# Attention scores as plain float32 products on the two row halves of the array

## The chip, the cores and the metric

The kernel runs on 1 core of one Trainium2 chip. The metric is the device time of one execution in microseconds (us). Most executions of a kernel agree within 0.3%. An engine here means one of TensorE (PE, matrix products; PEld is its weight load), VectorE (DVE), ScalarE (ACT), GpSimd (POOL); SP issues the large DMA transfers.

## The reference, cut to what matters

One layer of a hybrid backbone over 512 latent tokens of width 1024, with 256 context tokens. After an adaLN-modulated RMSNorm, one input projection feeds three groups of heads side by side: neighbourhood attention (8 heads of 64 dims), a Hyena mixer and a Conformer convolution module. Their outputs are concatenated, projected and added to the stream. Then follows a mixture of 16 experts in which every expert picks its 64 tokens.

```python
h  = modulate(rmsnorm(x, norm1_g), sh1, sc1)
q, k, v, hy_in, cf_in = split(h @ w_in)
kc, vc = split(modulate(rmsnorm(ctx, norm1_g), csh1, csc1) @ w_in[:, D_NA:3 * D_NA])
# per head, one softmax of a latent query over its grid window and all 256 context keys
s_nb = where(mask, einsum('bqhd,bkhd->bhqk', q, k) * 64 ** -0.5 + bias, -1e30)
s_cx = einsum('bqhd,bkhd->bhqk', q, kc) * 64 ** -0.5
p    = softmax(concat([s_nb, s_cx]))
attn = p[..., :nk] @ v + p[..., nk:] @ vc
x = x + g1 * (concat([attn, hyena(hy_in), conformer(cf_in)]) @ w_out)
h2 = modulate(rmsnorm(x, norm2_g), sh2, sc2)
x = x + g2 * expert_choice_ffn(h2, router_w, w1, w3, w2)     # w1, w3: 1024 x 2048, w2: 2048 x 1024, 16 experts
return rmsnorm(x, final_norm_g)
```

## The kernel before

The program runs once through these stages: adaLN vectors and norms; the projections for Hyena, the Conformer module, queries, values and keys, with the Hyena filter and the depthwise convolution beside them; attention, with the output projection of the other two groups as filler; the rest of the output projection, the second norm and the routing; 16 experts, whose weights (384 loads of 1 MB) come through a pool of 22 buffers of 1 MB (`U`); the final norm.

**Products in three parts.** Weights and activations are float32. For the projections each operand is split into a high part rounded to `float32r` and a low part, the rest; `mm3` (L547 to L550) then issues hi·hi, lo·hi and hi·lo, each one pass. `split` (L510) makes the parts of a weight block: ACT rounds (`wh`, L515), POOL or, for listed pieces, DVE subtracts (`wl`, L516). The experts' products (L1306, L1307, L1346) and the scatter product `pZ` (L1204) are plain float32: the compiler makes two matmul records of each.

**Queries and keys.** `evac_q` takes the projected queries out of the accumulation bank: per block m of two heads, ACT rounds each half of the rows (one head of 64 dims), scaled by -1/8, and DVE writes the rest to the *other* half of the rows (L727, L728). So the 128 rows of one head's stationary operand are its high and its low part. `dup_k` does the like for keys: ACT writes the high part to both halves of the rows (L733, L734), DVE the low part (L735). Keys take four buffers `KK` and one `kcl`, queries two `Q`.

**Scores.** `scores(hp, b, s)` makes the scores of one head (pair hp, half s) for 128 queries (block b): a matmul of 128 rows (high and low query against the doubled high key) and one of 64 rows (high query against low key), once for the 256 window keys and once for the 256 context keys: four matmuls (L946 to L949). Then DVE adds the bias and finds the minimum (L954), ACT takes exp with the sum (L957), DVE divides (L958, L959). `ptrans` transposes the 128x512 block in four matmuls into `pT` (L965) and copies it out as `PT`, in turn on ACT and DVE; `av` multiplies with the values into `pO` (L976) and splits the result into `mixh` (ACT, L980) and `mixl` (DVE, L981).

**What sets the order.** Around the attention the PE, ACT and DVE orders come from the scheduler of the tile framework, which places the program's instructions by its own estimate of when each can run and by the pools: four accumulation banks `psA` (projections `pP`, scores `pS`, output projection `pX`), two `psT`, two `psY`. The generator `attention` walks over 32 heads, two heads ahead of the transposes, and lets `out_part` fill in; from there on a string of words (L1140 in the kernel before) says when each step of the output projection, the routing and the rest of the attention is issued. SP's loads stand in one queue, in program order; a load that waits for its buffer holds up all loads behind it. `w_out` comes in four blocks: `load_wo(0, 1)` is called among the key products, `load_wo(n, 0)` multiplies the block by the gate on DVE (L880, four instructions of 128x512 each), and its attention half is used last. In the same stretch DVE runs the depthwise convolution as 60 multiply-adds (`glu`, L590); the copies of the context values (`vc`, L105) and the low parts of the key weights stand in the same DVE queue.

Of the kernel before, what the change touches and what calls it, by code (L numbers as in the profile page):

```python
# [9 lines left out]
FT = mybir.dt.float32  # L10
# [35 lines left out]
TYPE = [0, 1, 1, 2]  # L46
# [4 lines left out]
def hybrid_kernel(ctx: ExitStack, tc: tile.TileContext, a, out: bass.AP):  # L51
# [24 lines left out]
    def free(k=1, keep=0):  # L76
        used[0] -= k
        pump(keep)

    def free_only(k=1):  # L80
        used[0] -= k

    def psA(name="psA"):
        return psum.tile([128, 512], FT, name=name, tag="A", bufs=4)
# [7 lines left out]
    def W(name="w", dt=FT):  # L92
        if name in ("g", "aff2", "lists", "od", "sn", "u", "xo", "sig", "sq", "dg", "arg", ):
            return early.tile([128, 512], dt, name=name, tag="w", bufs=2)
        return work.tile([128, 512], dt, name=name, tag="w")
# [40 lines left out]
    def small_t(name, n, dt=FT, bufs=4):  # L136
        return work.tile([128, n], dt, name=name, tag=name, bufs=bufs)
# [28 lines left out]
    def take(key):  # L166
        while key not in ready:
            assert loads and used[0] < NU, key
            go = loads.popleft()
            if go is not None:  # L170
                go()
        return ready.pop(key)
# [337 lines left out]
    def split(raw, keep, dve=()):  # L510
        hi = U("wh", FR)
        lo = U("wl", FR)
        for i in range(4):
            s = slice(i * 512, (i + 1) * 512)
            nc.scalar.activation(hi[:, s], raw[:, s], AF.Copy)  # L515
            (nc.vector if i in dve else nc.gpsimd).tensor_sub(lo[:, s], raw[:, s], hi[:, s].bitcast(FT))  # L516
        free(1, keep)
        return hi, lo
# [200 lines left out]
    HALF = [slice(0, 64), slice(64, 128)]  # L719

    def evac_q(m, ps):
        if m % 2 == 0:
            Q.append(U("Q", FR))
        for s in range(2):
            r, o = HALF[s], HALF[1 - s]
            c = slice((2 * (m % 2) + s) * 512, (2 * (m % 2) + s + 1) * 512)
            nc.scalar.activation(Q[-1][r, c], ps[r], AF.Copy, scale=-0.125)  # L727
            nc.vector.scalar_tensor_tensor(Q[-1][o, c], ps[r], -0.125, Q[-1][r, c].bitcast(FT), op0=OP.mult, op1=OP.subtract)  # L728

    def dup_k(hi, lo, ps):  # L730
        for s in range(2):
            r, o = HALF[s], HALF[1 - s]
            nc.scalar.activation(hi[s][r], ps[r], AF.Copy)  # L733
            nc.scalar.activation(hi[s][o], ps[r], AF.Copy)  # L734
            nc.vector.tensor_sub(lo[r], ps[r], hi[s][r].bitcast(FT))  # L735

    def evac_k(m, ps):
        t = KK[m]
        dup_k([t[:, 0:512], t[:, 512:1024]], t[:, 1024:1536], ps)

    def evac_v(b, ps):
        if b == 0:
# [106 lines left out]
    def fetch_bias(hp):  # L849
        for s in range(2):  # L850
            rb[hp, s] = g = W("g")[:, 0:8 * RPBW]
            src = bass.AP(tensor=rp.tensor, offset=rp.offset + (2 * hp + s) * 15 * RPBW,
                          ap=[[1, 16], [RPBW, 8], [1, 7 * RPBW + 48]])
            nc.gpsimd.dma_start(g[:, 0:7 * RPBW + 48], src)
# [10 lines left out]

    parts = []
    for u in range(2):
        parts.append([t.rearrange("p (k n) -> p k n", n=512) for t in split(take(("win", "k", u)), 5, DVE_LO.get(("k", u), ()))])
    fetch_bias(0)
    build_tm(0)  # L870
    fetch_bias(1)
# [16 lines left out]
    for u in range(2):  # L888
        hi, lo = parts[u]
        if u:  # L890
            KK.extend([U("KK", FR) for _ in range(4)])
            kcl = U("kcl", FR)[:, 0:1024].rearrange("p (m n) -> p m n", n=256)
        for ctx_ in (True, False):
            for m in range(4):
                s = slice(m * 128, (m + 1) * 128)
                for k in range(4):
                    kg = 4 * u + k
                    mm3((psc if ctx_ else pss)[m], (hi[:, k, s], lo[:, k, s]),
                        (ch(kg), cl(kg)) if ctx_ else (hh(kg), hl(kg)), kg == 0, kg == 7)
                if u and ctx_:  # L900
                    dup_k([KK[m][:, 1536:1792], KK[m][:, 1792:2048]], kcl[:, m], psc[m])
                elif u:
                    evac_k(m, pss[m])
            if u and ctx_:
                free_only(2)
                load_wo(0, 1, 2)
        if u == 0:
            free_only(2)
# [27 lines left out]
    idxf = p1[0:16, 0:128].rearrange("e (i n) -> e i n", i=2)  # L936
    rsT = small.tile([128, 4], FT, name="rsT")

    def scores(hp, b, s):
        r = HALF[s]  # L940
        qt, kk = Q[hp // 2], KK[hp]
        q0 = (2 * (hp % 2) + s) * 512 + 128 * b
        q = qt[:, q0:q0 + 128]
        k0 = 8 * KB[b]
        ps = psA("pS")
        mm(ps[:, 0:256], q, kk[:, s * 512 + k0:s * 512 + k0 + 256], start=True, stop=False)  # L946
        mm(ps[:, 0:256], q[r], kk[r, 1024 + k0:1024 + k0 + 256], start=False, stop=True)
        mm(ps[:, 256:512], q, kk[:, 1536 + 256 * s:1792 + 256 * s], start=True, stop=False)
        mm(ps[:, 256:512], q[r], kcl[r, hp], start=False, stop=True)  # L949
        p = W("P")  # L950
        i = 2 * TYPE[b] + s
        m2 = small_t("m2", 4, bufs=6)

        nc.vector.tensor_tensor_reduce(out=p.rearrange("p (a n) -> p a n", a=2), in0=ps.rearrange("p (a n) -> p a n", a=2),  # L954
                                       in1=TM[hp][:, i:7:6 - i], scale=1.0, scalar=3e38,
                                       op0=OP.add, op1=OP.min, accum_out=m2[:, 0:1])
        nc.scalar.activation(p, p, AF.Exp, scale=-1.0, bias=m2[:, 0:1], accum_out=m2[:, 1:2])  # L957
        nc.vector.reciprocal(m2[:, 2:3], m2[:, 1:2])  # L958
        nc.vector.tensor_scalar(p, p, m2[:, 2:3], None, op0=OP.mult)  # L959
        return p  # L960

    def ptrans(p):
        t = psT("pT")
        for i in range(4):
            nc.tensor.transpose(t[:, i * 128:(i + 1) * 128], p[:, i * 128:(i + 1) * 128], ident)  # L965
        pt = W("PT")
        copy(pt, t)
        return pt
# [13 lines left out]

    def attention():
        ps = deque()
        pend = deque()
        steps = [(hp, b, s) for hp in range(2) for b in range(4) for s in range(2)]
        steps += [(hp, b, s) for b in range(4) for hp in (2, 3) for s in range(2)]
        parts = [out_part(0), out_part(1)]
        build_tm(1)
        fetch_bias(2)  # L990
        for i in range(len(steps) + 2):
            if i < len(steps):
                ps.append(scores(*steps[i]))
            for _ in range(2):
                if i < 8:
                    next(parts[0])
                elif 9 <= i < 17:
                    next(parts[1])
            if i >= 2:
                hp, b, s = steps[i - 2]  # L1000
                pend.append(ptrans(ps.popleft()))
                if s == 1:
                    av(b, hp, [pend.popleft(), pend.popleft()])
                    if b == 3:
                        free(2 + hp % 2, PK[hp])
                        if hp < 2:
                            build_tm(hp + 2)
                        if hp == 0:
                            fetch_bias(3)
                        if hp == 1:  # L1010
                            load_wo(0, 0, 2)
                            load_wo(1, 0, PK[4])
            if i == 7:
                finish(parts[0])
                free_only(2)
                load_wo(1, 1, PK[5])
            if i == 16:
                finish(parts[1])
                free_only(4)
            yield  # L1020

    def out_proj(n, b):
# [94 lines left out]
    limit[0] = 99  # L1117
    att = attention()
    ada3 = adaln(3)
    for i in range(26):  # L1120
        next(att)
        if i in (21, 21, 22, 25):
            next(ada3)

    def steps(g, at):
# [11 lines left out]
    left = lambda b: one(x_rows, b, 0)  # L1137
    go = lambda *g: [next(i, None) for i in g]
    op = {(n, b): out_proj(n, b) for n in range(2) for b in range(4)}
    for w in "p00 l0 p10 a a r0 a a p11 p01 r0 l1 r1 r0 r1 a p02 p12 q13 r1 r2 q13 r1 r0 a a q03 l2 q03 a f p13 r2 p03 r2 l3 r3 r3 r2 r3 r3".split():  # L1140
        if w == "a":
            go(att)
        elif w == "f":
            finish(att)
            free(3, 0)
        elif w[0] == "p":
            finish(op[int(w[1]), int(w[2])])
        elif w[0] == "q":
            go(op[int(w[1]), int(w[2])])
        elif w[0] == "l":  # L1150
            go(left(int(w[1])))
        elif w[0] == "r":
            go(rt[int(w[1])])
# [315 lines left out]
```

## Time and profile before

| quantity | value |
|---|---|
| median of 3 runs | 1385.86 us (1385.47 to 1389.58) |
| profiled execution | 1391.59 us, span 1389.8 us |
| mean granted TensorE clock in it | 0.958 of full speed |
| PE busy | 1280.8 us (92%) |
| DVE, ACT, POOL busy | 494.5, 229.6, 155.5 us |
| bytes moved by DMA | 458.02 MB |

The profile is of one execution. A busy PE is not PE at its peak: the records of matmuls overlap, so the time of one is read from the start of one record to the start of the next, or from the chain of waits. The granted clock is a share of 2.4 GHz; 0.5 is the lower level, 1.2 GHz. By place in the span: projections to about 268 us, attention from 268 to about 405 us, routing to about 432 us, experts to 1340 us, the final norm after that.

### The profile page before, as it was taken

How to read it: one execution, taken by the hardware profiler on the slowest of the kernel's cores; microseconds unless marked ns; L12 is line 12 of the kernel's file. 1: busy time of each engine (PE TensorE's matmuls, PEld its weight loads, DVE VectorE, ACT ScalarE, POOL GpSimd, SP SyncE). 2: the span in 40 equal slices, each digit the busy share in tenths (PEclk: the TensorE clock that was granted, in tenths of full speed). 3: DMA queues.
4: the chain of work that ended last, by engine and by line, in shares of the span. 5: the costliest groups of instructions: out<-in, count | busy, mean ns of one | idle time of the engine just before them, and what ended most of it. 6: DMA issues, size and time to landing. Idle time of an engine off the chain costs nothing.

```text
span 1389.8 us, 15284 instructions
## 1 busy us (share of the span) xinstructions
PE 1280.8 (92%) x6148; PEld 625.6 (45%) x6148; DVE 494.5 (36%) x991; ACT 229.6 (17%) x477; POOL 155.5 (11%) x166
## 2 busy tenths in 40 slices
PE   6998888999988998998999999899899889989987
PEld 2576566776663335334333433533433353343323
DVE  6777997485464111112112121211212121121214
ACT  3532232743440101000000000100000010000002
POOL 2333443455020000000000000000000000000000
PEclk9999998997999997998999899899999989999999
DMA  9835022432457996999999999999999999999996
GB/s 354 339 145 188 31 65 80 120 120 91 181 214 303 416 414 259 416 421 414 417 417 414 421 413 421 415 417 418 414 421 414 419 416 417 417 415 421 414 419 268
DMA packets 89365, 458.02 MB, mean 330 GB/s; under 512 B 7364, under 2 KB 9228, under 8 KB 54478
## 3 DMA queue, kind: packets, MB, share of 16 engines
q1 hardware_dynamic: 88046, 453.64, 81.1%
q0 software_dynamic: 912, 3.06, 0.9%
q8 instruction: 48, 0.79, 0.2%
q10 hardware_dynamic: 336, 0.35, 0.1%
q14 instruction: 23, 0.19, 0.0%
HBM read 453.87 MB, written 2.36 MB: 328 GB/s over the span
## 4 chain that ended last, share of the span: by engine, by line
PE 70%; DVE 13%; DMA 11%; ACT 3%; issue 2%; POOLq 0%; DVEq 0%; ACTq 0%; SPq 0%
PE pa L1306 26%; PE py L1346 13%; DMA ld<-in_w_dram 10%; PE pT L1194 7%; PE pZ L1204 4%; DVE glu L590 4%; PE pT L1333 2%; PE pO L976 2%; PE pa L1307 1%; PE pP L550 1%; PE pP L549 1%; PE pP L548 1%; PE pM L431 1%; PE pT L965 1%; PE pX L548 1%
## 5 line engine op out<-in xcount | busy, mean ns | idle before, releaser
L1307 PE MATMUL pa<-ld,xh 128*64 128x512 f32 x1024 | 455.5, 595 | 10.2 <-DMA ld<-in_w_dram 10.2
L1306 PE MATMUL pa<-ld,xh 128*64 128x512 f32 x1024 | 455.8, 595 | 0.3 <-DVE xh L1088 0.3
L1306 PEld LDWEIGHTS pa<-ld,xh 128*64 128x64 f32 x1024 | 135.0, 137 | 262.2 <-issue 256.1
L1346 PE MATMUL py<-ld,xh 128*64 128x512 f32 x1024 | 225.0, 597 | 0.0
L1207 DVE TENSOR_TENSOR acc<-acc,pZ 128x512 f32<-128x512 f32 x112 | 72.0, 684 | 307.2 <-PE pZ L1204 307.2
L1307 PEld LDWEIGHTS pa<-ld,xh 128*64 128x64 f32 x1024 | 134.9, 137 | 47.7 <-issue 26.5
L1346 PEld LDWEIGHTS py<-ld,xh 128*64 128x64 f32 x1024 | 72.5, 138 | 141.1 <-issue 137.5
L103 ACT ACTIVATE au<-pa 128x512 f32<-128x512 f32 x32 | 19.1, 597 | 641.6 <-PE pa L1307 641.6
L1194 PE MATMUL pT<-ohg,ld 128*128 128x128 f32 x512 | 95.8, 347 | 31.1 <-DVE xh L1088 15.1
L1373 POOL DMA_INDIRECT out_dram<-yg,where x1 | 1.1, 1115 | 953.0 <-DVE yg L1372 953.0
L1194 PEld LDWEIGHTS pT<-ohg,ld 128*128 128x128 f32 x512 | 82.5, 242 | 48.2 <-DVE xh L1088 21.7
L1350 DVE SCALAR_TENSOR_TENSOR yg<-py,ig,g1bc 128x512 f32<-128x512 f32 x16 | 12.0, 752 | 206.6 <-PE py L1346 206.6
L516 POOL TENSOR_TENSOR wl<-ld,wh 128x512 fp32r<-128x512 f32 x44 | 62.7, 1454 | 95.6 <-ACT wh L515 71.3
L1204 PE MATMUL pZ<-yg,oh 64*128 64x512 f32 x240 | 68.9, 641 | 1.5 <-DVE acc L1207 1.5
L548 PE MATMUL pP<-hh,wh 128*128 128x512 f32 x144 | 60.3, 420 | 7.8 <-DVE vc L105 6.6
L549 PE MATMUL pP<-hl,wh 128*128 128x512 f32 x144 | 58.9, 410 | 1.5 <-DVE hl L507 1.5
L550 PE MATMUL pP<-hh,wl 128*128 128x512 f32 x144 | 57.6, 410 | 2.7 <-DVE wl L516 2.7
L590 DVE SCALAR_TENSOR_TENSOR glu<-glu,p 128x512 f32<-128x512 f32 x60 | 57.9, 965 | 1.1
L1333 PE MATMUL pT<-c,au 128*128 128x128 f32 x256 | 41.8, 292 | 12.3 <-DVE acc L1207 5.4
L1088 DVE TENSOR_SCALAR xh<-pT,A,B 128x128 f32<-128x128 f32 x32 | 13.1, 410 | 106.5 <-PE pT L1194 106.5
L105 DVE COPY au<-pa 128x512 f32<-128x512 f32 x32 | 22.1, 692 | 76.0 <-PE pa L1307 72.9
L1333 PEld LDWEIGHTS pT<-c,au 128*128 128x128 f32 x256 | 28.6, 146 | 29.9 <-DVE xh L1336 13.1
(345 smaller groups left out, 1371.9 us busy)
## 6 DMA issues: line engine op xcount, KB each, us to landing
ld<-in_w_dram SPq DMA_DIRECT2D x384, 1024.0 KB, 19.8
ld<-in_w_mod_dram SPq DMA_DIRECT2D x24, 1024.0 KB, 11.4
ld<-in_w_in_dram SPq DMA_DIRECT2D x11, 1024.0 KB, 6.3
ld<-in_w_out_dram SPq DMA_DIRECT2D x4, 1024.0 KB, 9.0
ld<-in_x_dram SPq DMA_DIRECT2D x2, 1024.0 KB, 12.7
ld<-in_x_dram SPq DMA_DIRECT2D x4, 512.0 KB, 7.0
out_dram<-acc SPq DMA_DIRECT2D x4, 512.0 KB, 9.9
g<-in_rpb_dram POOLq DMA_DIRECT2D x8, 244.5 KB, 3.6
```

The lines of the kernel that those rows point to most:

```text
L516: (nc.vector if i in dve else nc.gpsimd).tensor_sub(lo[:, s], raw[:, s], hi[:, s].bitcast(FT))
L548: mm(ps, l[0], r[0], start=start, stop=False)
L549: mm(ps, l[0], r[1], start=False, stop=False)
L550: return mm(ps, l[1], r[0], start=False, stop=stop)
L590: nc.vector.scalar_tensor_tensor(yc[i], glt[i][:, j:j + 512], cw[:, i, j:j + 1], yc[i], op0=OP.mult, op1=OP.add)
L1194: mm(pk, xblk(b)[:, k * 128:(k + 1) * 128], g[:, b * 128:(b + 1) * 128], start=(b == 0), stop=(b == 3))
L1204: mm(ps[h], oh[pr, 128 * c:128 * c + 128], yg[pr], start=True, stop=True)
L1207: nc.vector.tensor_add(ablk(c)[:, s], (ablk if e else xblk)(c)[:, s], ps[h])
L1306: mm(pa[f][0:64], xT[:, k, cs], w1[:, s], start=(k == 0), stop=(k == 7))
L1307: mm(pa[f][64:128], xT[:, k, cs], w3[:, s], start=(k == 0), stop=(k == 7))
L1333: nc.tensor.transpose(p[:, i * 128:(i + 1) * 128], au[f][:, i * 128:(i + 1) * 128], ident)
L1346: mm(py[64 * h:64 * h + 64], hT[:, f], w2[:, i * 1024 + 512 * h:i * 1024 + 512 * h + 512], start=(f == 0), stop=(f == 15))
```

## The change

Queries are copied out once, as plain float32, by ACT (four instructions of 128x512). Keys are copied once per block of two heads, window keys and context keys, by `copy`, which takes ACT and DVE in turn. The two heads of a pair lie on the two halves of the rows of these tiles. The scores of a pair are two plain float32 matmuls, each with 64 rows and 512 columns (256 window keys and 256 context keys through one strided operand), one on each half of the rows. `attention` walks over 16 pairs instead of 32 heads, one pair ahead of the transposes. Q takes one buffer instead of two, KK two instead of four, `kcl` is gone; the counts of buffers freed and kept follow. Softmax, transposes and the products with the values are as before.

```diff
     def evac_q(m, ps):
-        if m % 2 == 0:
-            Q.append(U("Q", FR))
-        for s in range(2):
-            r, o = HALF[s], HALF[1 - s]
-            c = slice((2 * (m % 2) + s) * 512, (2 * (m % 2) + s + 1) * 512)
-            nc.scalar.activation(Q[-1][r, c], ps[r], AF.Copy, scale=-0.125)
-            nc.vector.scalar_tensor_tensor(Q[-1][o, c], ps[r], -0.125, Q[-1][r, c].bitcast(FT), op0=OP.mult, op1=OP.subtract)
-
-    def dup_k(hi, lo, ps):
-        for s in range(2):
-            r, o = HALF[s], HALF[1 - s]
-            nc.scalar.activation(hi[s][r], ps[r], AF.Copy)
-            nc.scalar.activation(hi[s][o], ps[r], AF.Copy)
-            nc.vector.tensor_sub(lo[r], ps[r], hi[s][r].bitcast(FT))
-
-    def evac_k(m, ps):
-        t = KK[m]
-        dup_k([t[:, 0:512], t[:, 512:1024]], t[:, 1024:1536], ps)
+        if m == 0:
+            Q.append(v512(U("Q")))
+        nc.scalar.activation(Q[0][:, m], ps, AF.Copy, scale=-0.125)
+
+    kat = lambda m: KK[m // 2][:, 768 * (m % 2):768 * (m % 2) + 768]
...
-            KK.extend([U("KK", FR) for _ in range(4)])
-            kcl = U("kcl", FR)[:, 0:1024].rearrange("p (m n) -> p m n", n=256)
+            KK.extend([U("KK") for _ in range(2)])
...
-                    dup_k([KK[m][:, 1536:1792], KK[m][:, 1792:2048]], kcl[:, m], psc[m])
+                    copy(kat(m)[:, 512:768], psc[m])
                 elif u:
-                    evac_k(m, pss[m])
+                    copy(kat(m)[:, 0:512], pss[m])
...
-    def scores(hp, b, s):
-        r = HALF[s]
-        qt, kk = Q[hp // 2], KK[hp]
-        q0 = (2 * (hp % 2) + s) * 512 + 128 * b
-        q = qt[:, q0:q0 + 128]
+    def scores(hp, b):
+
         k0 = 8 * KB[b]
-        ps = psA("pS")
-        mm(ps[:, 0:256], q, kk[:, s * 512 + k0:s * 512 + k0 + 256], start=True, stop=False)
-        mm(ps[:, 0:256], q[r], kk[r, 1024 + k0:1024 + k0 + 256], start=False, stop=True)
-        mm(ps[:, 256:512], q, kk[:, 1536 + 256 * s:1792 + 256 * s], start=True, stop=False)
-        mm(ps[:, 256:512], q[r], kcl[r, hp], start=False, stop=True)
...
+        o = 768 * (hp % 2) + k0
+        kk = KK[hp // 2][:, o:o + 2 * (512 - k0)].rearrange("p (a n) -> p a n", a=2)[:, :, 0:256]
+        pss = [psA("pS") for _ in range(2)]
+        for s in range(2):
+            mm(pss[s].rearrange("p (a n) -> p a n", a=2), Q[0][HALF[s], hp, 128 * b:128 * b + 128], kk[HALF[s]],
+               start=True, stop=True)
...
-        steps = [(hp, b, s) for hp in range(2) for b in range(4) for s in range(2)]
-        steps += [(hp, b, s) for b in range(4) for hp in (2, 3) for s in range(2)]
+        steps = [(hp, b) for hp in range(2) for b in range(4)] + [(hp, b) for b in range(4) for hp in (2, 3)]
...
-        for i in range(len(steps) + 2):
+        for i in range(len(steps) + 1):
...
-                        free(2 + hp % 2, PK[hp])
...
+                    free((1, 2, 1, 3)[hp], PK[hp])
```

The change also moves instructions. On PE, at the start of the attention (`pP` are the last key products, `pX` the output projection that fills in), there stand before the four matmuls of a head:

```order
719 L550 MATMUL pP<-hh,wl 128x512
720 L946 MATMUL pS<-KK,Q 128x256
721 L947 MATMUL pS<-KK,Q 128x256
722 L948 MATMUL pS<-KK,Q 128x256
723 L949 MATMUL pS<-kcl,Q 128x256
724 L548 MATMUL pX<-wh,mixh_1177 128x512
```

and after it a pair of heads in one row of two:

```order
724 L550 MATMUL pP<-hh,wl 128x512
725 L932 MATMUL pS<-KK,Q 128x512 x2
726 L548 MATMUL pX<-wh,mixh_1174 128x512
727 L549 MATMUL pX<-wl,mixh_1174 128x512
728 L550 MATMUL pX<-wh,mixl_1175 128x512
729 L548 MATMUL pX<-wh,mixh_1174 128x512
```

Ten of the 16 pairs stand so, both matmuls in a row; of the other six, the two matmuls stand apart, with other products between them.

On DVE, at the end of the depthwise convolution (`glu`) and before the key products, there stand before:

```order
222 L590 SCALAR_TENSOR_TENSOR glu<-glu,p_70 128x512 x11
223 L105 COPY vc_1476<-pC 128x512
224 L590 SCALAR_TENSOR_TENSOR glu<-glu,p_70 128x512 x2
225 L516 TENSOR_TENSOR wl<-ld,wh 128x512
226 L590 SCALAR_TENSOR_TENSOR glu<-glu,p_70 128x512
227 L516 TENSOR_TENSOR wl<-ld,wh 128x512
```

and after:

```order
211 L590 SCALAR_TENSOR_TENSOR glu<-glu,p_70 128x512 x12
212 L105 COPY vc_1463<-pC 128x512
213 L516 TENSOR_TENSOR wl<-ld,wh 128x512
214 L590 SCALAR_TENSOR_TENSOR glu<-glu,p_70 128x512
215 L459 COPY mT<-pT 128x4x4
216 L516 TENSOR_TENSOR wl<-ld,wh 128x512
```

Of the four multiply-adds that stood behind the copy of `vc`, three now stand ahead of it, and the eight L728 that stood earlier in this queue are gone.

On DVE, around the first softmaxes (L954 before, L940 after, is the bias and the minimum; L880 before, L867 after, multiplies `w_out` by the gate), there stand before, behind the first three L954:

```order
267 L735 TENSOR_TENSOR KK<-pP,KK 64x512
268 L958 RECIPROCAL m_1999<-m_1999 128x1
269 L958 RECIPROCAL m_2016<-m_2016 128x1
270 L959 TENSOR_SCALAR P<-P,m_1999 128x512
271 L959 TENSOR_SCALAR P<-P,m_2016 128x512
272 L880 TENSOR_TENSOR ld<-ld,g1bc 128x512
273 L954 ISA P,m_2044<-pS,tm 128x512
```

and after:

```order
237 L562 TENSOR_TENSOR mixl_1175<-glu,mixh_1174 128x512 x2
238 L105 COPY KK<-pC 128x256
239 L105 COPY KK<-pP 128x512
240 L867 TENSOR_TENSOR ld<-ld,g1bc 128x512 x8
241 L105 COPY KK<-pP 128x512
242 L940 ISA P,m_1932<-pS,tm 128x512
```

The eight gate products now stand in one row ahead of the first softmax, instead of spread over the first heads.

## Rows read from the trace of the kernel before

**Rows 1.** The page: busy time of PE, and the chain that ended last.
```profile
PE 1280.8 (92%) x6148; PEld 625.6 (45%) x6148; DVE 494.5 (36%) x991; ACT 229.6 (17%) x477; POOL 155.5 (11%) x166
PE 70%; DVE 13%; DMA 11%; ACT 3%; issue 2%; POOLq 0%; DVEq 0%; ACTq 0%; SPq 0%
```

**Rows 2.** Stretches: busy us (instructions) per engine; then clock, DMA share, GB/s.
```profile
150.00:230.00 80.00, 64.90 (x315) 47.55 (x313) 78.81 (x119) 24.90 (x48) 36.54 (x30) 0.98 0.25 76
230.00:270.00 40.00, 39.59 (x208) 33.48 (x208) 18.26 (x42) 18.19 (x33) 7.96 (x12) 0.92 0.24 52
...
230.00:240.00 10.00, 9.86 (x39) 8.09 (x40) 5.76 (x10) 0.00 (x0) 0.00 (x0) 0.69 0.00 0
...
270.00:330.00 60.00, 59.36 (x318) 41.45 (x318) 44.64 (x97) 30.66 (x69) 36.84 (x40) 1.00 0.36 118
330.00:346.00 16.00, 16.00 (x68) 9.44 (x70) 8.08 (x19) 3.37 (x9) 10.89 (x9) 0.56 0.36 147
346.00:405.00 59.00, 58.91 (x377) 39.97 (x375) 27.19 (x79) 24.04 (x64) 8.40 (x30) 0.98 0.39 146
430.00:440.00 10.00, 8.93 (x46) 4.95 (x48) 4.29 (x20) 0.46 (x1) 1.05 (x1) 1.00 0.24 94
550.00:1340.00 790.00, 742.18 (x3436) 291.80 (x3432) 144.08 (x264) 47.08 (x104) 0.00 (x0) 0.97 1.02 417
```

**Rows 3.** Waits of PE from 150 to 275 us: total, times, longest.
```profile
PE pP L548 <- DVE vc L105: 6.6, 1, 6.6
```

**Rows 4.** DVE in order of time, 215 to 263 us: start, length, line, idle before.
```profile
217.24 12.24 DVE L590 SCALAR_TENSOR_TENSOR glu<-glu,p 128x512 f32<-128x512 f32 x11
229.40 0.68 DVE L105 COPY vc<-pC 128x512 f32<-128x512 f32 x1
...
233.98 1.28 DVE L516 TENSOR_TENSOR wl<-ld,wh 128x512 fp32r<-128x512 f32 x2
...
260.52 2.12 DVE L562 TENSOR_TENSOR mixl<-glu,mixh 128x512 fp32r<-128x512 f32 x2 [1.91 <-ACT mixh L561]
```

**Rows 5.** Query and key splits: min/median/max ns, first to last start us.
```profile
L728 DVE SCALAR_TENSOR_TENSOR Q<-pP,Q x8: 683/685/694, 168.5 to 190.9; 64x512 fp32r<-64x512 f32 x8
L735 DVE TENSOR_TENSOR KK<-pP,KK x8: 682/688/695, 254.7 to 279.1; 64x512 fp32r<-64x512 f32 x8
```

**Rows 6.** The chain of waits from 330 to 346 us: start, us.
```profile
331.54 0.31 PE pS L947
...
332.32 0.51 PE pS L949
```

**Rows 7.** PE in order of time: two of `pX`, then scatter products of experts.
```profile
308.23 0.39 PE L548 MATMUL pX<-wh,mixh 128*128 128x512 f32 x1
308.46 0.40 PE L549 MATMUL pX<-wl,mixh 128*128 128x512 f32 x1
...
497.43 1.13 PE L1204 MATMUL pZ<-yg,oh 64*128 64x512 f32 x4
498.49 0.64 PE L1306 MATMUL pa<-ld,xh 128*64 128x512 f32 x1
...
1338.44 1.72 PE L1204 MATMUL pZ<-yg,oh 64*128 64x512 f32 x4 [0.77 <-DVE acc L1207]
```

**Rows 8.** The chain of waits from 225 to 310 us: one float32 matmul alone.
```profile
238.56 0.86 PE pL L598 x2
```

**Rows 9.** Softmax and gate products: min/median/max ns, first to last start.
```profile
L954 DVE CUSTOM_DVE_ANT_1 P<-pS,tm x28: 672/680/692, 271.9 to 397.3; 128x512 f32<-128x512 f32 x28
L957 ACT ACTIVATE P<-P,m x32: 708/717/727, 275.8 to 402.6; 128x512 f32<-128x512 f32 x32
L959 DVE TENSOR_SCALAR P<-P,m x32: 477/487/1549, 276.8 to 403.6; 128x512 f32<-128x512 f32 x32
L880 DVE TENSOR_TENSOR ld<-ld,g1bc x8: 665/684/1267, 281.0 to 303.5; 128x512 f32<-128x512 f32 x8
```

**Rows 10.** DMA issues: count, KB each, median us to landing.
```profile
ld<-in_w_out_dram SPq DMA_DIRECT2D x4, 1024.0 KB, 9.0
```

More of the change, by code (lines that the diff above doesn't have):

```diff
@@ L867, in hybrid_kernel @@
     for u in range(2):
-        parts.append([t.rearrange("p (k n) -> p k n", n=512) for t in split(take(("win", "k", u)), 5, DVE_LO.get(("k", u), ()))])
+        parts.append([t.rearrange("p (k n) -> p k n", n=512) for t in split(take(("win", "k", u)), 2, DVE_LO.get(("k", u), ()))])
     fetch_bias(0)
@@ L937, in hybrid_kernel @@
     rsT = small.tile([128, 4], FT, name="rsT")
-    def scores(hp, b, s):
-        r = HALF[s]
-        qt, kk = Q[hp // 2], KK[hp]
-        q0 = (2 * (hp % 2) + s) * 512 + 128 * b
-        q = qt[:, q0:q0 + 128]
-        k0 = 8 * KB[b]
-        ps = psA("pS")
-        mm(ps[:, 0:256], q, kk[:, s * 512 + k0:s * 512 + k0 + 256], start=True, stop=False)
-        mm(ps[:, 0:256], q[r], kk[r, 1024 + k0:1024 + k0 + 256], start=False, stop=True)
-        mm(ps[:, 256:512], q, kk[:, 1536 + 256 * s:1792 + 256 * s], start=True, stop=False)
-        mm(ps[:, 256:512], q[r], kcl[r, hp], start=False, stop=True)
[L950 to L960, printed above, removed]
@@ new lines, in scores @@
+    def scores(hp, b):
+        k0 = 8 * KB[b]
+        o = 768 * (hp % 2) + k0
[4 more added lines that the diff above has]
+               start=True, stop=True)
+        out = []
+        for s, ps in enumerate(pss):
+            p = W("P")
+            i = 2 * TYPE[b] + s
+            m2 = small_t("m2", 4, bufs=6)
+            nc.vector.tensor_tensor_reduce(out=p.rearrange("p (a n) -> p a n", a=2), in0=ps.rearrange("p (a n) -> p a n", a=2),
+                                           in1=TM[hp][:, i:7:6 - i], scale=1.0, scalar=3e38,
+                                           op0=OP.add, op1=OP.min, accum_out=m2[:, 0:1])
+            nc.scalar.activation(p, p, AF.Exp, scale=-1.0, bias=m2[:, 0:1], accum_out=m2[:, 1:2])
+            nc.vector.reciprocal(m2[:, 2:3], m2[:, 1:2])
+            nc.vector.tensor_scalar(p, p, m2[:, 2:3], None, op0=OP.mult)
+            out.append(p)
+        return out
@@ L984, in attention @@
         ps = deque()
-        pend = deque()
-        steps = [(hp, b, s) for hp in range(2) for b in range(4) for s in range(2)]
-        steps += [(hp, b, s) for b in range(4) for hp in (2, 3) for s in range(2)]
+        steps = [(hp, b) for hp in range(2) for b in range(4)] + [(hp, b) for b in range(4) for hp in (2, 3)]
         parts = [out_part(0), out_part(1)]
@@ L990, in attention @@
         fetch_bias(2)
-        for i in range(len(steps) + 2):
+        for i in range(len(steps) + 1):
             if i < len(steps):
                 ps.append(scores(*steps[i]))
-            for _ in range(2):
-                if i < 8:
+            for _ in range(4):
+                if i < 4:
                     next(parts[0])
-                elif 9 <= i < 17:
+                elif 5 <= i < 9:
                     next(parts[1])
[L999 to L1004, printed above, removed]
-                        free(2 + hp % 2, PK[hp])
[L1006 to L1013, printed above, removed]
+            if i == 8:
+                finish(parts[1])
+                free_only(4)
+            if i >= 1:
+                hp, b = steps[i - 1]
+                av(b, hp, [ptrans(p) for p in ps.popleft()])
+                if b == 3:
+                    free((1, 2, 1, 3)[hp], PK[hp])
+                    if hp < 2:
+                        build_tm(hp + 2)
+                    if hp == 0:
+                        fetch_bias(3)
+                    if hp == 1:
+                        load_wo(0, 0, 2)
+                        load_wo(1, 0, PK[4])
+            if i == 3:
                 finish(parts[0])
@@ L1016, in attention @@
                 load_wo(1, 1, PK[5])
-            if i == 16:
-                finish(parts[1])
-                free_only(4)
             yield
@@ L1119, in hybrid_kernel @@
     ada3 = adaln(3)
-    for i in range(26):
+    for i in range(13):
         next(att)
-        if i in (21, 21, 22, 25):
+        if i >= 10:
             next(ada3)
@@ L1139, in hybrid_kernel @@
     op = {(n, b): out_proj(n, b) for n in range(2) for b in range(4)}
-    for w in "p00 l0 p10 a a r0 a a p11 p01 r0 l1 r1 r0 r1 a p02 p12 q13 r1 r2 q13 r1 r0 a a q03 l2 q03 a f p13 r2 p03 r2 l3 r3 r3 r2 r3 r3".split():
+    for w in "p00 l0 p10 a r0 a p11 p01 r0 l1 r1 r0 r1 a p02 p12 q13 r1 r2 q13 r1 r0 q03 l2 q03 a f p13 r2 p03 r2 l3 r3 r3 r2 r3 r3".split():
         if w == "a":
@@ L1144, in hybrid_kernel @@
             finish(att)
-            free(3, 0)
+            free(2, 0)
         elif w[0] == "p":
```

## The prediction

> **What bounds the kernel now.** I read the page first: PE is busy for 92% of the span and holds 70% of the chain that ended last, DVE 13%, DMA 11% [rows 1]. That is an average, so the table of stretches comes next [rows 2]. It shows four regimes. From 150 to 230 us DVE is busy 78.81 of 80 us and PE 64.90: DVE bounds. From 230 to 405 us PE is busy nearly throughout (39.59 of 40, 59.36 of 60, 16.00 of 16, 58.91 of 59), at full clock but for 330 to 346, where 0.56 was granted, about the lower level: PE bounds. At 430 to 440 the DMA share falls to 0.24: the buffers are full before the experts begin, so the stream waits for the experts' start. From 550 to 1340 the DMA share is 1.02 at 417 GB/s: the weight stream bounds, and it has no gap in which to make up time. So what is gained before the experts' start should move the end by as much, and what is lost too. The third view is PE's waits (one only is large: 6.6 us for the `vc` copy on DVE [rows 3]), the fourth the order in time on DVE and PE.
>
> The sum is made on the profiled execution, 1391.59 us (span 1389.8 and 1.8 around it). It lies 5.7 above the median, 1385.86; I take the same difference for both.
>
> **Part 1: queries without a low part.** Eight L728 of 685 ns leave DVE [rows 5]: 5.5 us, all between 168 and 191 us, inside the stretch where DVE hardly idles, so all of it is on the path. The convolution then ends 5.5 us earlier. The order adds something: PE's key products began at 230.1, when the `vc` copy, held up behind eleven multiply-adds, was done [rows 3, 4]. Three of the four later multiply-adds now stand ahead of that copy, but the key products now begin with the context ones (`pC`), which need no bank that `vc` frees; what they do need are the `wl` pieces, which DVE finished at 235.3 and now finishes 5.5 earlier, the first of them right behind the copy. I take 6.5 us (1 to 9: one if PE finds another wait at once, since its work from 150 us has 15 us of slack; nine if the low clock of the first key products, part of the 0.92 in 230 to 270, goes with the gap).
>
> **Part 2: keys copied once.** L733 to L735 leave ACT and DVE; on PE nothing falls, since PE is busy 39.59 of 40 us there. I count 0. ACT's and DVE's time in this stretch is cover for the next part.
>
> **Part 3: the scores on PE.** Before, 32 heads of four matmuls, each 0.31 us from start to start at full clock and 0.51 at the low one [rows 6]: 128 x 0.31 = 39.7 us. After, 16 pairs of two float32 matmuls of 64 rows and 512 columns. The kernel has this very form elsewhere: `pZ`, 64 rows by 512 columns, two on the two row halves, took 1.06 us from its start to the next product's (497.43 to 498.49) [rows 7]. A float32 matmul of 512 columns on 128 rows, alone, takes 0.86 [rows 8], so the halves do run beside each other. Ten pairs stand together in the new order, 10 x 1.06 = 10.6. Six pairs stand apart: 12 lone matmuls; no row has one of 64 rows alone, the nearest are 0.86 and, for a `pZ` pair whose second matmul had to wait, 1.72 for two (at 1338.44) [rows 7, 8]. I take 0.93: 11.2. Sum 21.8, so 18 us less. Bounds: all pairs side by side 16 x 1.06 = 17, 23 less; all one after the other 32 x 1.0 = 32, 8 less.
>
> The Trainium skill has a rule that speaks against this: "FP8 and Floating Point Precision", section TensorE Precision Notes, says that true float32 takes four passes through the array, where the kernel before made three. Worked out from that as an estimate, 512 columns at 2.4 GHz are 0.85 us a matmul, which agrees with the 0.86 of the lone one, and two in turn would be 1.7. The Trainium skill, "TensorEngine Tiling (Array Packing)", section Tiling Modes, adds that tiles work in parallel, which agrees with 1.06, and that a change of mode drains the engine. By the first rule alone the scores would be 27 us and 12 would be gained; the rows decide for 18.
>
> **Part 4: what PE then waits for.** PE's time shrinks, the softmax doesn't. From 270 to 330 DVE is busy 44.64 of 60 us [rows 2]. 22 of the 32 heads lie before 333 us, by a count of the `pS` records up to the one at 332.32 [rows 6], so PE's time there falls by about 22/32 x 18 = 12 us, to some 47; DVE's by five L735 of 0.69 to some 41. So both come near full, and the order on each is fixed. The start is the tightest place: the eight gate products now stand ahead of the first softmax, 8 x 0.68 = 5.5 us [rows 9], behind a load of 9.0 us [rows 10] that is issued after `mixl`, at 262.6 before [rows 4]. Behind them on DVE wait all softmaxes, and behind those the transposes on PE. PE has two pairs and 24 products `pX` to do meanwhile, about 2 x 1.06 + 24 x 0.23 (start to start) [rows 7] = 7.6 us; the way is the rest of the load, 5.5 us and one softmax (0.68 + 0.72 + 0.49 and the small ones, about 2.5). If `mixl` comes 8 us earlier than before, about 254, the load lands at 264, the gate products end at 269.5 and the first transpose can start at 272; PE would be through its filler at 261.5 + 7.6 = 269. I take 3 us here and 3 for the latency of later pairs where filler is short, 6 in all (1 to 15). In before nothing of this cost PE anything: 59.36 of 60.
>
> **Part 5: behind the attention.** Routing begins when the output projection ends; nothing in it changes. Four buffers fewer let weights in sooner, but the stream halts at 430 to 440 anyway with all buffers full: 0, and no loss. The low clock of 330 to 346 cost about 7 of 16 us; whether it returns I can't tell from one execution: 0, 7 either way.
>
> Sum: -6.5 - 18 + 6 = -18.5. On the profiled execution 1391.59 - 18.5 = 1373; on the median, 1385.86 - 18.5 = 1367.
>
> **Rivals.**
> A. *The halves don't help.* In most places the second score matmul waits for a bank or for the weight load, and pairs cost 1.7 to 2.0. For: six pairs stand apart, and four banks `psA` serve both scores and `pX`. Against: ten pairs stand together, and 240 `pZ` ran so. Then 8 to 12 us on PE, less idling since PE is slower: -6.5 - 9 + 4 = -11.5, 1374.
> B. *The softmax becomes the bound.* DVE has 41 us to do in the first 47 and ACT some 25, in a chain that goes back and forth between them; if PE idles for one exp (0.72) [rows 9] in each of 16 pairs, that is 11.5, with the 3 at the start 14.5 instead of 6. Against: PE idles 0.6 of 60 us there before [rows 2]. -6.5 - 18 + 14.5 = -10, 1376. The Trainium skill, "TensorEngine Tiling (Array Packing)", section PSUM Bottleneck, warns of this: tiling speeds up the products but not the copies out of the banks. The trace of before can't show it, as its scores are slow enough to hide the copies.
> C. *Slower.* PE now idles in the attention, and with idle the granted clock falls to its lower level; in before it was 0.69 from 230 to 240 us, right after PE's 6.6 us of idle time [rows 2, 3]. At 0.5 every us of PE work costs two. The gain of 18.5 is gone when 18.5 us of work run at the lower level beyond the 9 us of work that did so in 330 to 346; at 25 us or more, which is half of the work from 346 to 405, the time is 1385.86 + 6.5 = 1392. For: it happened for 16 us with PE fully busy. Against: 58.91 of 59 busy at 0.98 right after.
> D. *Nothing comes of it.* The stream of weights, not the experts' start, sets the end: then only the earlier buffers count, and the time is 1382 to 1386. Against: the hole at 430 to 440.
>
> **How the numbers follow.** The forecast has 0.56, A 0.14, B 0.16, C 0.07, D 0.07. About 0.3%, 4.2 us, is what a measurement can tell from no change. Faster by more than that (below 1381.7): the forecast, A and B, 0.86; D gives mostly the same, with a little of C and of the forecast's tail, 0.08; slower 0.06. The range: low end from the good bounds of two terms (23 for the scores, 9 for the projections, stalls of 1: -31, of which I take half beyond the forecast), 1353; high end past A and B, 1380, leaving out C and most of D.
>
> **What would show it.** Right: key products that start near 224 us; `pS` pairs of about 1.06 us; PE busy share from 262 us on falling to some 90%, with waits for `PT` and the softmax; a DMA hole before the experts that shifts with them; the last expert 18 us earlier. Wrong: pairs at 1.7 or more (A); DVE over 90% busy in the attention (B); long stretches at 0.5 to 0.6 granted (C); the experts' stream reaching its end at the old time (D).

## The result, and the profile after

The changed kernel takes 1372.03 us (median of 4 runs, 1369.08 to 1374.3) against 1385.66 (4 runs): ratio 0.9884, 95% interval 0.9856 to 0.9912. Run again it gave 0.9874 (0.9854 to 0.9895). So it is 14 to 18 us faster, by the medians and the ratios of both; 1367 was forecast, with 1353 to 1380 as the range.

The page of the profiled execution (1374.3 us, span 1372.4) shows little of it, as averages do:

```profile
PE 1267.0 (92%) x6084; PEld 614.1 (45%) x6084; DVE 491.7 (36%) x971; ACT 213.8 (16%) x445; POOL 154.4 (11%) x166
PE 69%; DVE 14%; DMA 13%; issue 2%; ACT 1%; POOLq 0%; DVEq 0%; SPq 0%; ACTq 0%
```

The table of stretches (columns as in [rows 2]) does:

```profile
150.00:230.00 80.00, 70.27 (x330) 52.81 (x328) 79.11 (x113) 22.79 (x45) 37.78 (x30) 0.96 0.28 80
270.00:280.00 10.00, 6.25 (x14) 3.94 (x15) 9.61 (x20) 3.04 (x8) 3.13 (x4) 0.66 0.55 182
280.00:346.00 66.00, 66.00 (x410) 38.59 (x410) 48.92 (x114) 30.29 (x74) 36.51 (x35) 1.00 0.37 134
346.00:405.00 59.00, 52.22 (x356) 35.66 (x355) 34.26 (x121) 23.35 (x65) 11.54 (x41) 0.95 0.47 178
410.00:420.00 10.00, 7.91 (x30) 4.40 (x30) 6.92 (x32) 0.00 (x0) 1.05 (x1) 0.83 0.31 124
550.00:1340.00 790.00, 746.89 (x3422) 301.20 (x3420) 145.36 (x270) 47.49 (x105) 0.00 (x0) 0.95 1.02 417
```

PE is busier from 150 to 230 us, 70.27 of 80 us against 64.90 [rows 2]. A hole is new at 270 to 280 (6.25 of 10, clock 0.66), where before had none. The DMA hole ahead of the experts is still there, at 410 to 420 instead of 430 to 440, and the stream of the experts runs at the same 417 GB/s.

The spans between landmarks, read from the starts of PE's records, in both executions of the changed kernel:

| from, to (us) | before | after | after, again |
|---|---|---|---|
| first projection product `pP` | at 50.5 | at 52.1 | at 50.5 |
| from there to the first score product | 217.6 | 213.3 | 213.7 |
| from there to the end of the last `pX` (attention) | 143.0 | 127.4 | 127.0 |
| from there to the first expert product (routing) | 23.6 | 25.2 | 24.6 |
| from there to the end of the last `py` (experts) | 945.8 | 945.2 | 947.3 |

The projections gave 4, the attention 16, the routing took 1 to 2 back, and the experts' time did not change beyond what two executions differ by. From the first projection product on the traces differ by 19.0 and 17.3 us, more than the runs' 14 to 18: the profiled execution of before lies 5.7 us above its median. The first row is how much an execution starts early or late; it belongs to neither kernel.

Within the attention, PE's time by tile (from the start of one record to the start of the next, and the gaps) went from 41.9 to 24.4 for `pS`, from 17.5 to 20.4 for the transposes `pT` (the step into a product on the row halves is 0.20 and counts there), from 7.9 to 5.6 for `pM`, from 23.3 to 21.0 for `pO`, and idle time from 1.0 to 4.4. `pM` (the products of the adaLN vectors) and `pO` are unchanged in number; before, part of them ran in the 16 us at 0.56 [rows 2].

A pair of score products on the two row halves, in order of time on PE, has the step that `pZ` had [rows 7]; then a transpose and the matmul of a head that stands alone, in two records:

```profile
281.48 1.13 PE L932 MATMUL pS<-KK,Q 64*128 64x512 f32 x4
282.54 0.50 PE L548 MATMUL pX<-wh,mixh 128*128 128x512 f32 x1
...
298.51 0.66 PE L952 MATMUL pT<-c,P 128*128 128x128 f32 x4
299.10 1.12 PE L932 MATMUL pS<-KK,Q 64*128 64x512 f32 x2
300.15 0.50 PE L548 MATMUL pX<-wh,mixh 128*128 128x512 f32 x1
```

From 281.48 to 282.54 are 1.06 us for two matmuls (four records); from 299.10 to 300.15 are 1.05 for one (two records). A lone matmul costs as much as a pair. The trace so agrees with the Trainium skill, "TensorEngine Tiling (Array Packing)", section Tiling Modes, that tiles work in parallel.

The hole at 270 to 280 on DVE (start, length, line, and the idle time before with what ended it), and the longest of PE's waits from 150 to 420 us:

```profile
263.69 2.50 DVE L867 TENSOR_TENSOR ld<-ld,g1bc 128x512 f32<-128x512 f32 x4 [2.94 <-DMA ld<-in_w_out_dram]
267.90 5.19 DVE L867 TENSOR_TENSOR ld<-ld,g1bc 128x512 f32<-128x512 f32 x4 [1.71 <-DMA ld<-in_w_out_dram]
273.01 0.68 DVE L105 COPY KK<-pP 128x512 f32<-128x512 f32 x1
```

```profile
PE pS L932 <- DVE KK L105: 4.3, 1, 4.3
```

The two loads of `w_out` arrive at 263.7 and 267.9; the eight gate products wait for them, twice, and end at 273.1; the last key copy stands behind them, and PE's second score pair behind that. The wait for `vc` [rows 3] is gone.

In the rest of the attention PE idled 0.1 us in all.

### The profile page after: what moved, and what is told of

It is laid out like the page before. It is cut to its first block, busy times and chain, and to the rows that moved or that the text cites. A ratio compares the mean times of both kernels' runs of the same rounds, so it can differ in the third digit from the quotient of the medians.

```text
span 1372.4 us, 15073 instructions
## 1 busy us (share of the span) xinstructions
PE 1267.0 (92%) x6084; PEld 614.1 (45%) x6084; DVE 491.7 (36%) x971; ACT 213.8 (16%) x445; POOL 154.4 (11%) x166
## 4 chain that ended last, share of the span: by engine, by line
PE 69%; DVE 14%; DMA 13%; issue 2%; ACT 1%; POOLq 0%; DVEq 0%; SPq 0%; ACTq 0%
PE pa L1290 25%; PE py L1330 12%; DMA ld<-in_w_dram 11%; PE pT L1178 7%; DVE glu L590 4%; PE pZ L1188 4%; PE pT L1317 2%; PE pS L932 2%; PE pO L963 2%; PE pP L550 1%; PE pT L952 1%; PE pM L431 1%; PE pP L549 1%; PE pP L548 1%; PE pa L1291 1%
## 5 line engine op out<-in xcount | busy, mean ns | idle before, releaser
L1178 PE MATMUL pT<-ohg,ld 128*128 128x128 f32 x512 | 101.7, 363 | 31.4 <-DVE xh L1072 15.5
L1178 PEld LDWEIGHTS pT<-ohg,ld 128*128 128x128 f32 x512 | 87.6, 256 | 49.1 <-DVE xh L1072 22.4
```

The source lines that it names most:

```text
L1178: mm(pk, xblk(b)[:, k * 128:(k + 1) * 128], g[:, b * 128:(b + 1) * 128], start=(b == 0), stop=(b == 3))
```

## The experiments

Each ratio is to the kernel before, on the same chip. To compare: the changed kernel has 0.9884 and 0.9874. One thousandth is 1.4 us.

**1. Both heads on one row half.** Scores of the second head are those of the first, so the output is not the reference's; the order of all engines is as in the changed kernel.

```diff
-            mm(pss[s]..., Q[0][HALF[s], hp, 128 * b:128 * b + 128], kk[HALF[s]],
+            mm(pss[s]..., Q[0][HALF[0], hp, 128 * b:128 * b + 128], kk[HALF[0]],
```

> The changed kernel with one difference: both score matmuls of a pair read the first head's row half of Q and K (so the second head's scores are a copy of the first's and the output is not the reference's). The order of all engines is the same; only the row half differs. Theory (the row halves work side by side, and PE's time for the scores lies on the path): the ten pairs that stand together take 1.7 to 1.9 us instead of 1.06, the lone matmuls stay at 1.05, so PE needs 10 x 0.7 = 7 us more and the time rises by 5 to 8 us over the changed kernel, 1377 to 1380. Rival (the score time on PE is hidden behind the softmax, the gain came from the fewer copies): pairs get longer, the time does not move, 1372 within 3.

Measured: 1381.26, ratio 0.9949 (0.9932 to 0.9966), 9 to 10 us more than the changed kernel, where 5 to 8 were expected. The chain of waits (start, us) shows a pair, which took 1.06, at 1.91:

```profile
280.00 1.91 PE pS L932 x4
```

The lone ones stayed at 1.05; `pS` took 33.1 us in all, 8.8 more, and the attention 136.2, 9 more. So the row halves do work side by side, and PE's time for the scores is on the path, one for one.

**2. One pass a score matmul.** Q and K are rounded to `float32r`; their low parts are left out.

```diff
-            Q.append(v512(U("Q")))
+            Q.append(v512(U("Q", FR)))
-            KK.extend([U("KK") for _ in range(2)])
+            KK.extend([U("KK", FR) for _ in range(2)])
```

> The changed kernel with Q and K rounded to float32r, so that a score matmul is one pass instead of two records of plain float32 (the low parts of queries and keys are left out). Theory (PE bounds the attention): a group of scores falls from 1.05 to about 0.5 us, 20 groups, so 8 to 11 us less than the changed kernel, 1361 to 1364. Rival (DVE's softmax bounds the attention by now): PE's time falls, its idle time rises by as much, 1372 within 3.

Measured: 1361.18, ratio 0.9799 (0.9775 to 0.9823), 11 us less than the changed kernel. `pS` fell by 15.4 us to 8.9 and the attention by 13.6 to 113.6; a pair or a lone matmul takes 0.43. PE's time is given back at nearly nine tenths, so DVE doesn't bound the attention as a whole even here. A pair in the chain of waits, and the wait for the key copy, which stayed:

```profile
280.56 0.43 PE pS L932
...
PE pS L932 <- DVE KK L105: 4.6, 1, 4.6
```

**3. The gate products among the later softmaxes.**

```diff
+    late = []
...
             for k in range(4):
+                col = w[:, 512 * k:512 * k + 1]
+                nc.vector.scalar_tensor_tensor(col, late[1 + 4 * n + k][:, 0:1], 0.0, col, op0=OP.mult, op1=OP.add)
                 nc.vector.tensor_mul(v512(w)[:, k], v512(w)[:, k], g1bc[:, n * 512:(n + 1) * 512])
...
+                late.append(ps[-1][1])
```

`late` holds a probability tile of each pair, as they come.

> The changed kernel, with each of the eight gate products of w_out tied behind the softmax of one of the pairs 1 to 8 by a one-column operation that adds zero times a probability; they then stand singly among the softmaxes and not in a row ahead of the first. Theory (the gate products and their DMA hold up the last key copy and the first softmax): PE's idle 4.3 us at the second pair and the low clock after it (0.66 from 270 to 280) go, 5 to 8 us less than the changed kernel: 1364 to 1367. Rival (the start of the attention is hidden by something later, or the gate products cost as much among the later softmaxes): 1372 within 3.

Measured: 1368.59, ratio 0.9866 (0.9845 to 0.9887): by its interval not apart from the changed kernel, and short of the 5 to 8 us that were expected. In the trace the attention was 122.2 us, 5 shorter, and the routing 26.8, 2 longer. It was run again:

> The kernel with the gate products tied behind the softmaxes of pairs 1 to 8 once more. In its first trace the attention was 5 us shorter than in the changed kernel, the routing 2 us longer, and the time 0.9866 of before against 0.9884 and 0.9874 of the changed kernel. If the 5 us are kept: 0.984 to 0.986. If most of them are lost again behind the attention: 0.986 to 0.988, as in the first run.

Measured: 1364.56, ratio 0.9845 (0.9814 to 0.9877), the attention 122.2 again, the routing 25.2. The longest of PE's waits from 255 to 390 us there:

```profile
PE pT L1026 <- DVE ld L1017: 1.7, 1, 1.7
```

The wait for the key copy is gone, and the attention is 5 us shorter in both traces: the gate products were the hole. Of the time, the middle of both runs is 3 us less than the changed kernel's; the second run alone falls where the 5 us are kept. Whether 3 or 5 remain, the intervals don't tell.

**4. The eight DVE instructions put back.** The changed kernel makes the queries' low part again, into a tile that nobody reads.

```diff
         nc.scalar.activation(Q[0][:, m], ps, AF.Copy, scale=-0.125)
+        qlo = W("qlo")
+        for s in range(2):
+            r, o = HALF[s], HALF[1 - s]
+            nc.vector.scalar_tensor_tensor(qlo[o], ps[r], -0.125, Q[0][r, m], op0=OP.mult, op1=OP.subtract)
```

> The changed kernel with the eight DVE instructions of 64x512 that made the queries' low part put back, into a work tile that nobody reads. Theory (DVE bounds the stretch from 150 to 230 us, so each of its us there moves the end): 4 to 6 us more than the changed kernel, 1376 to 1378, and key products that end 4 to 6 us later. Rival (the traces show the key products end only 2.7 us earlier, so something else bounds): 0 to 2 us more.

Measured: 1372.12, ratio 0.9892 (0.9873 to 0.9911): one or two thousandths (1 to 2.5 us) above the changed kernel and inside its interval. DVE did get them back: its last `wl` piece came 184.8 us after the first projection product, as before (184.7), where the changed kernel has it at 180.9 and 181.4. But the first score product came after 213.0 us, as without them (213.3, 213.7). So the theory did not hold; runs 5 and 6 put the question to the kernel before. The run is not just the changed kernel with that work added: the scheduler made another order of PE's projections from it. A part of the wait for `vc` is back, and the wait for the key copy fell to 1.2 us.

```profile
PE pP L548 <- DVE vc L105: 2.5, 1, 2.5
```

The attention took 126.9 us, as in the changed kernel. So the run shows that the DVE work need not cost time where the order is made with it; what it costs in the changed kernel's own order stays open.

**5. The kernel before without that DVE work.** The low part of the queries is left out; a second copy of the high part, by ACT, stands in its place.

```diff
-            nc.vector.scalar_tensor_tensor(Q[-1][o, c], ps[r], -0.125, Q[-1][r, c].bitcast(FT), op0=OP.mult, op1=OP.subtract)
+            nc.scalar.activation(Q[-1][o, c], ps[r], AF.Copy, scale=-0.125)
```

> The kernel before, with the eight DVE instructions for the queries' low part replaced by second copies on ACT (so the low part is left out and a copy of the high part stands in its place). Theory 1 (DVE's 5.5 us themselves are the gain of the projections): 4 to 6 us less than before. Theory 2 (after putting those eight back into the changed kernel cost nothing, the gain of the projections is the place of the vc copy and of the first key products): only as much as the new order happens to shorten PE's wait of 6.6 us for vc; the order here has seven multiply-adds ahead of that copy and none behind, so the wait shrinks as well and 2 to 5 us less than before. Both give a gain; the trace tells them apart: by theory 1 the key products end earlier by 5.5 us, by theory 2 by what PE's wait for vc loses.

Measured: 1380.94, ratio 0.9937 (0.9914 to 0.9959), 9 us less than before and more than either theory gave. The first score product came after 212.2 us, 5.4 earlier. The rest was the attention, 136.6 against 143.0: there was no stretch like that from 330 to 346 us at the low clock. The stretch at the same place, with the clock at 1.00:

```profile
330.00:340.00 10.00, 10.00 (x71) 4.93 (x70) 6.31 (x16) 2.44 (x7) 5.31 (x5) 1.00 0.31 100
```

**6. The kernel before with the `vc` copies on ACT.** DVE keeps its eight instructions.

```diff
-                    copy(vc[j], ps)
+                    alt[0] ^= 1
+                    nc.scalar.activation(vc[j], ps, AF.Copy)
```

> The kernel before, with the two copies of the context values made on ACT instead of one of them on DVE; DVE keeps the eight low parts of the queries. Theory 2 (PE's wait of 6.6 us for that copy, behind eleven multiply-adds, held the key products): the wait goes and the key products end 3 to 5 us earlier, 3 to 5 us less than before. Theory 1 (DVE's work itself bounds): DVE loses only the 0.7 us of the copy, and the time falls by no more than 1 us.

Measured: 1389.54, ratio 1.0005 (0.9987 to 1.0024): nothing. The wait for `vc` was gone and the first score product came 3.1 us earlier (214.5), but new waits for `wl` took its place in part,

```profile
PE pC L550 <- DVE wl L516: 3.0, 2, 2.5
```

and the attention took 146.1 instead of 143.0, with the clock below full from 270 to 300 (0.89) and from 320 to 350 (0.83).

**7. The buffers held.** Three more buffers are kept until the softmax of the last pair.

```diff
+            hold = [U("hold") for _ in range(3)]
+            for t in hold:
+                nc.gpsimd.memset(t[:, 0:4], 0.0)
...
+                if i == 15:
+                    for t in hold:
+                        nc.vector.scalar_tensor_tensor(t[:, 0:4], ps[-1][1][:, 0:4], 0.0, t[:, 0:4], op0=OP.mult, op1=OP.add)
...
-            free(2, 0)
+            free(5, 0)
```

> The changed kernel, with three buffers of 1 MB taken when the keys are and held until the softmax of the last pair, so that (with the one of Q, which stays free) the pool is nearly as full as before. Theory (part 5 of the prediction: the stream fills all buffers before the experts begin anyway): within 2 us of the changed kernel, 0.986 to 0.990 of before. Rival (the four buffers let expert weights in sooner, and that is part of the gain): 3 MB at 417 GB/s are 7.5 us, 4 to 7.5 us more than the changed kernel, 0.991 to 0.993.

Measured: 1372.9, ratio 0.9891 (0.9861 to 0.9921): as the changed kernel. The DMA hole ahead of the experts is there as well. The freed buffers gave nothing.

**8. One pass and late gate products together.** The edits of 2 and 3 (the low parts of queries and keys are left out).

> The changed kernel with both edits of the runs before: the gate products tied behind the softmaxes of pairs 1 to 8, and Q and K rounded to float32r with one pass a score matmul (the low parts of queries and keys are left out). Theory (both are on PE's path and don't overlap, as one pass left the wait of 4.6 us for the key copy in place): the two gains add, 0.980 - 0.002 to 0.005 of before, 0.975 to 0.978. Rival (with PE's work down to that, DVE's softmax bounds the attention, and the gate products cost there what they save at the start): 0.980 as with one pass alone.

Measured: 1359.73, ratio 0.9763 (0.9738 to 0.9788), the fastest of all; the middle lies 5 us below one pass alone, though the intervals overlap. In the one trace the attention is no shorter (114.1 against 113.6) and PE waits elsewhere: it is busy 6.12 of 10 us from 280 to 290. So whether the gains add is open.

The changed kernel once more, on the chip of runs 5, 6 and 8:

> The changed kernel once more, unchanged, on the chip of the three that follow: 0.988 of the kernel before. In its trace the key products should end about 4 to 6 us earlier than before, counted from the first projection product, and PE should wait at the second score pair for the key copy behind the gate products.

It came out nearly as expected: 1373.8 us, ratio 0.9874, the first score product 3.8 us earlier (4 to 6 were expected), and

```profile
PE pS L932 <- DVE KK L105: 4.2, 1, 4.2
```

## Why the prediction was right, and where its terms were off

**The sum.** -18.5 was forecast; the medians show -13.6 and -15.6, the ratios -16 and -17.5. The place was right too: the attention gives most of it, and the experts' start hands it on unchanged (945.8 against 945.2 and 947.3). That the traces' -19.0 and -17.3 come so near to the sum is in part luck: terms were off both ways, as told under parts 1, 3, 4 and 5. The low end of the range, 1353, does not come out of its own terms: -31 from the median is 1355, and half of what lies beyond the forecast is 1361.

**Part 3, the scores.** The mechanism held. The pair at 1.06 was read off `pZ` and came at 1.06. Lone matmuls were taken at 0.93, between the rows; they cost 1.05, so that standing apart saves nothing on a pair, and six pairs cost twice. `pS` fell by 17.5 us against 18, but so close a figure is luck: the 41.9 of before hold matmuls at the low clock, which the sum (39.7) left out, and the 24.4 one pair at it (2.6 us). Where the scores ran at full clock they took 39.3 before (run 5, all but a few) and 23.4 after (run 3), 16 us less. The transposes beside them rose by 2.9, a term that the sum lacked; the step from a transpose into a score product is 0.20, where it was 0.03. Run 1 shows rival A's price, 9 us, and that it did not come; run 2 shows the slope. The four passes that the Trainium skill gives for true float32 ("FP8 and Floating Point Precision", section TensorE Precision Notes), by the prediction's estimate 0.85 us a matmul, agree with the 0.86 that the second matmul on one half adds in run 1 (1.91 less 1.05), not with the 1.05 of a lone one.

Side by side is not the whole saving. With both heads on one half the scores took 33.2 us, still less than the 39.3 of the old code. What remains can be read from the steps. In the kernel before, score matmuls of 128 and of 64 rows take turns, 0.31 us apart; the context key products, one pass of 256 columns as well but of 128 rows throughout, stand 0.12 apart:

```profile
293.48 0.36 PE L946 MATMUL pS<-KK,Q 128*128 128x256 f32 x1
293.78 0.38 PE L947 MATMUL pS<-KK,Q 64*128 64x256 f32 x1
...
237.09 0.28 PE L548 MATMUL pC<-hch,wh 128*128 128x256 f32 x1
237.21 0.28 PE L549 MATMUL pC<-hcl,wh 128*128 128x256 f32 x1
```

So about 0.19 of the 0.31 seems to go with the change of rows. In the changed kernel such a surplus of 0.2 is there once a group, however many matmuls stand in it; the chain of waits has two pairs in a row at 1.92, which is 1.06 and 0.86:

```profile
326.52 1.92 PE pS L932 x8
```

As an estimate from these steps: before, 128 x 0.19 = 24 us of surplus and 128 x 0.12 = 15 of products; after, 20 groups, 20 x 0.2 = 4, and 22 steps of 0.86 = 19. Fewer changes of rows would then be worth 20 us and the products cost 4 more; without the halves side by side they would cost another 9. The 9 are shown by run 1; the 20 are not, as no run changes the order of 128 and 64 rows alone.

**Part 4, the waits.** 6 us were forecast, 3 of them at the start. Idle time rose by 3.4 us, with one wait of 4.3 and little else, at the place named and for the cause named: gate products behind their loads. What PE waited for was the last key copy in the same queue, not the first transpose; the prediction had listed only softmaxes behind them. The low clock that followed cost the pair at 273.75 another 1.6 us, and the products `pX` after it 0.43 a step instead of 0.23. The second 3 us, latency later on, did not come, nor did two of its signs: PE was busy 122.95 of 127.35 us, not some 90%, and did not wait for `PT`. Run 3 shows the hole was worth 5 us of attention. A reading was off too, without harm: by the records 19 heads lie before 333 us, not 22, so PE's time to 330 us falls by 11, not 12.

**Part 1, the projections.** This is the term that was off: 6.5 forecast, 4.3 and 3.8 measured (6.0 in the trace of run 1, which has the same order up to there). The step that failed is "all of it is on the path": the 5.5 us came off DVE (its last `wl` 3 to 4 us earlier), but put back in run 4 they cost 1 to 2.5 us by the ratios and nothing at the first score product. What the runs show in its place is PE's idle time between the first projection product and the first score product: 20.8 us before, 16.0 and 17.2 after, 17.0 in run 4, 15.2 in run 5, 18.4 in run 6. With the new key code the schedule fills PE's waits even with DVE as late as before, in an order of its own; with the old code, the fewer instructions on DVE do it (run 5), and the `vc` copy alone does less (run 6: 3.1 us of the 5.4, of which the time shows nothing). These are single traces: the two executions of run 3's kernel differ by 2.1 us at the first score product (212.2 and 210.2). The step on the order was misread as well: key products did not begin at 230.1, for the first context one ran at 221.5 before and at 224.4 after, so that their start "near 224 us" told nothing. Which edit of the change frees the order is not settled: no run has the new queries with the old keys.

**Part 5.** The buffers were worth nothing, as forecast (run 7). Routing took 1 to 2 us more in both traces, which was not forecast. The low clock of 330 to 346 us was left at 0; the changed kernel did not show it, and the kernel of run 5, without it, was 6 us faster in the attention. That run 6 shows a like stretch speaks for it being a part of the old order's time, but with one profile of the kernel before, how often it comes there is open, and so is whether some 5 us of the gain are due to its absence. Beside run 5, which has the old scores without that stretch, the changed kernel's attention is 9 us shorter and not 16 (`pS` 15 less, transposes and idle time 3 more each), where the sum had 12: the rest of the 16 in the traces is a term that the prediction left at 0.

**Rivals.** A (the halves don't help): no, by run 1. B (softmax bound): no, PE's time in the attention is passed on at nine tenths (run 2). C (idle PE at the low clock): it happened, at 0.66 from 270 to 280 us, and then no more in the attention's next 66 us. D (hidden by the stream): no, the end came as much earlier as the experts' start, within what two executions differ by.

## What to carry to other kernels

When a product is moved to another form, look for a place in the same trace that has the form already: its step, from the start of one record to the start of the next product, came out to the hundredth. What a shorter engine then waits for is decided by the order of the others: look there for blocks that are early only because nothing held them, here eight gate products waiting on a load ahead of a copy that PE needed. And a queue that is full for 80 us isn't for that alone the bound: only taking its work away and giving it back, in each order, tells. Products that alternate between two forms are worth a look too: compare their step with that of like products among their own kind.

## What the runs showed of the hardware

A float32 matmul of 64 rows and 512 columns costs 1.05 us alone and 1.06 with a second one on the other row half; two on the same half cost 1.91, and two pairs in a row 1.92. In one pass a lone matmul or a pair costs 0.43, where one of 128 rows among its like takes 0.23 [rows 7]. So a group on the row halves cost some 0.2 us above its products in either precision, once a group; what the 0.2 are made of, no run shows. That a lone half is no cheaper than two was not in any row of before.
